# Eight modulation sums tied behind the score scalings of heads three and four, and three convolution tiles paced over the blocks of three heads, in a one-core decoder layer

## The chip, the cores and the metric

The kernel runs on one core of a Trainium2 chip. The core has five engines with queues of their own that work at the same time: TensorE (PE in the profile) multiplies matrices into PSUM, VectorE (DVE), ScalarE (ACT) and GpSimd (POOL) work on tiles, and SyncE (SP) only issues loads and stores. ScalarE's queue issues loads as well. Each engine takes its instructions in a fixed order; an instruction waits for semaphores of other engines or of a load. The metric is the device time of one execution in microseconds.

## The reference

One decoder layer on 512 positions of 1024 channels: a conditioned mixer and a conditioned convolutional feed-forward part. Cut to what matters here:

```python
cond = jax.nn.silu(c)
mod = cond @ ada_w[l] + ada_b[l]                      # 6 x 1024 modulation values
sh1, sc1, g1, sh2, sc2, g2 = jnp.split(mod[:, None, :], N_MOD, axis=-1)
u = rms_norm(x, mix_pre_g[l]) * (1.0 + sc1) + sh1
proj = u @ w_in[l]                                    # q, k, v, o, gates, glu
...
h = mlstm_chunkwise(heads(q), heads(k), heads(v), ...)          # 4 heads of 256
h = rms_norm(h, ml_norm_g[l].reshape(H, Dh)).reshape(Bsz, S, D_ML)
h = (h * jax.nn.sigmoid(o_pre)).astype(x.dtype)
y = causal_dwconv(a * jax.nn.sigmoid(gt), cv_dw_w[l], cv_dw_b[l])   # 31 taps
y = jax.nn.silu(layer_norm(y, cv_ln_g[l], cv_ln_b[l]))
mix = jnp.concatenate([h, y], axis=-1) @ w_out[l]
x = x + g1 * rms_norm(mix, mix_post_g[l])
```

The change touches how the 1024 values of `g1` are computed in time (eight blocks of 128) and when the depthwise convolution `y` is computed (eight tiles of 128 channels, 31 taps each). Both results stay what they were.

## The kernel before

All tensors lie with channels on 128 partitions and the 512 positions along the free axis; a product is made of three matrix multiplies of high and low parts (`mm3`, L201), so TensorE has most of the work. Its order is written out by hand: the glu projections, the value projection of head 0, the six projections q, q, k, k, o, o of head 0 (`head_proj`, tiles `qko`), and then a loop over h = 0, 1, 2 in which the attention of head h is laced with the projections of head h + 1. After the loop come the attention of head 3 laced with the first half of the output projection (`mixa`), its second half (`mixb`), and the feed-forward part (`up`, `dn`). The order on SyncE is by hand too. On VectorE, ScalarE and GpSimd a planner places the instructions by their priorities (work under `tc.cur_priority += LATER` comes when the engine has nothing more urgent) and by the order ties that the code adds (`behind`, and the dependency inside `ada_block`). An order tie is no wait of its own: it only says which of two instructions comes first on the engine.

The names that the prediction uses:

- `attention(h)` is a generator. It makes the four score blocks `s` (L519), which VectorE multiplies into the decay tiles `E` (L520, "score scaling"; `last_e[0]` holds the latest one), then the four outputs `o` (L530), which ScalarE copies out to `hn` (L534). VectorE scales `hn` by `fac` (L548), for which GpSimd computes a power (`fac`, L545). After that the two transposes `hT` (L554) go through PSUM, and VectorE multiplies them into `so` (L556). Scores, outputs and transposes share two PSUM banks (`atbank`), so each next one waits until the one before the last has been read out. The transposes of heads 0 and 1 are made one head later, between the first and the second pair of scores.
- `conv_tile(j)` makes one convolution tile: 25 taps on VectorE (L735, tiles `cv`), five taps on ScalarE and GpSimd (`cs`, L729 and L731), then the copy to `gt` (L742), an addition on GpSimd (L744), and the running mean and squares (`ydl`, `ysum`, `ysq`). The first `FREE` tiles are laid out whole at low priority. The others come through `pace()`, five taps at a time, each fifth tap tied behind the latest scaling or projection tap.
- `ada_block(i, behind)` makes one modulation sum: ScalarE's queue issues a load of 512 KB (L165, tiles `ada`, two buffers in turn), and VectorE multiplies it by the condition and sums along the row into `mod` (L167, the discarded product is called `junk`). A load into one of the two buffers waits for the sum that read it two blocks earlier. Blocks 16 to 23 are `g1`; `gain(0, ...)` uses them.
- `norm_rows()` normalises the eight convolution tiles: VectorE multiplies (L795), ScalarE applies silu (L796) and makes the high part `yh` (L798), VectorE makes the low part `yl` (L799).

Of the kernel before, what the change touches and what calls it, by code (L numbers as in the profile page):

```python
# [20 lines left out]
KT = D // P  # L21
# [6 lines left out]
LATER = 100000  # L28
# [26 lines left out]
def decoder_layer(ctx, tc, w_glu0, x, c, adaT, vecs, w_glu, w_qko, w_v0, w_v, w_out, w_up, w_down, out):  # L55
# [115 lines left out]
    def ada_done(a, b):  # L171
        V.tensor_tensor(out=mod[:, a:b], in0=mod[:, a:b], in1=vcols("ada_b", a, b - a), op=ALU.add)
# [320 lines left out]
    def head_proj(h, i):  # L493

        pieces, qs, ks, so = heads[h]
        ps = mmbank(f"qko{h}_{i}")
        proj(ps, pieces, i * KT)
        e = 2 * h + i % 2
        if i < 2:
            qs.append(conv4(ps, e, f"q{h}_{i}"))  # L500
        elif i < 4:
            ks.append(conv4(ps, 8 + e, f"k{h}_{i}"))
        else:
            t = slot(f"so{h}_{i}")
            S.activation(t, ps, AF.Tanh, scale=0.5)
            so.append(t)

    last_lo = [None]
    last_e = [None]
# [156 lines left out]
    def gain(i, first, g):  # L666
        V.scalar_tensor_tensor(out=gains[:, i * KT : (i + 1) * KT], in0=mod[:, first : first + KT], scalar=RD, in1=vcols(g, 0, KT),
                               op0=ALU.mult, op1=ALU.mult)
# [45 lines left out]
        tc.add_manual_dep(ins.ins, anchor.ins.name, mybir.DependencyInfo(mybir.DependencyClass.NoSync, mybir.DependencyReason.DATA),  # L714
                          reason="order on an engine")

    last_tap = [None, None]

    def conv_tile(j, every=CK):

        cp = cvbank(f"cv{j}")
        w = lambda tap: cvw[:, tap * KT + j : tap * KT + j + 1]
        S.activation(cp, cvx[j], AF.Identity, bias=vcol("cv_dw_b", j), scale=w(CK - 1))  # L723
        side = None
        for d in range(1, SIDE + 1):
            t = cvs.tile([P, T], F32, tag="cvs", name=f"cs{j}_{d}")
            if d == 1:
                V.memset(t[:, :d], 0.0)
            S.activation(t[:, d:], cvx[j][:, : T - d], AF.Copy, scale=w(CK - 1 - d))  # L729
            if side is not None:  # L730
                G.tensor_tensor(out=side[:, d:], in0=side[:, d:], in1=t[:, d:], op=ALU.add)  # L731
            else:
                side = t
        for n, d in enumerate(range(SIDE + 1, CK)):
            tap = V.scalar_tensor_tensor(out=cp[:, d:], in0=cvx[j][:, : T - d], scalar=w(CK - 1 - d), in1=cp[:, d:], op0=ALU.mult, op1=ALU.add)  # L735
            if every < CK and n % every == 0:
                behind(tap, last_e[0])
            last_tap[j // (KT - 1)] = tap
            if (n + 1) % every == 0 and d < CK - 1:
                yield  # L740
        y = cvx[j]
        S.activation(y, cp, AF.Copy)  # L742
        if side is not None:
            G.tensor_tensor(out=y, in0=y, in1=side, op=ALU.add)  # L744
        ys[j] = y

        if j:
            mean_of = ys[0] if j == 1 else ysum
            dl = cvtile(f"ydl{j}")
            V.scalar_tensor_tensor(out=dl, in0=mean_of, scalar=-1.0 / j, in1=y, op0=ALU.mult, op1=ALU.add)  # L750
            dst = ysq if j == 1 else dl
            S.activation(dst, dl, AF.Square, scale=(j / (j + 1.0)) ** 0.5)
            if j > 1:
                G.tensor_tensor(out=ysq, in0=ysq, in1=dl, op=ALU.add)
            G.tensor_tensor(out=ysum, in0=mean_of, in1=y, op=ALU.add)

    FREE = 6
    tc.cur_priority += LATER
    for j in range(FREE):
        for _ in conv_tile(j):  # L760
# [10 lines left out]
    def pace():  # L771
        tc.cur_priority += LATER
        next(paced, None)
        tc.cur_priority -= LATER
# [27 lines left out]
    for h in range(H - 1):  # L802
        head_load(h + 1)
        steps = attention(h)
        if h == 0:
            head_proj(1, 0)
        next(steps)
        head_proj(h + 1, 1 if h == 0 else 0)
        if h:
            pace()  # L810
            for _ in turns:
                pass
        next(steps)
        if h:
            pace()
            head_proj(h + 1, 1)
            pace()
        head_proj(h + 1, 2)
        if h:
            pace()  # L820
        next(steps)
        head_proj(h + 1, 3)
        if h:
            pace()
        next(steps)
        if h:
            pace()
        head_proj(h + 1, 4)
        next(steps)
        if h:  # L830
            pace()
        head_proj(h + 1, 5)
        make_E(h + 1)
        if h == H - 2:
            norm_mean()
        values = make_v(h + 1)
        next(values)
        next(values)
        if h < H - 2:
            turns = steps  # L840
        else:
            for _ in steps:
                pass
        if h == H - 2:
            norm_sums()

    tc.cur_priority += LATER
    for i in range(16, 24):
        ada_block(i, last_tap[0])
    ada_done(16, 24)  # L850
    tc.cur_priority -= LATER
    gain(0, 16, "mix_post_g")
    wo = {}
    steps = attention(H - 1)
    next(steps)
    mix_first(0)
    next(steps)
    norm_rows()
    mix_first(1)
    mix_first(2)  # L860
# [212 lines left out]
    for i in range(NF):  # L1073
# [29 lines left out]
        else:  # L1103
# [5 lines left out]
            if i % 2:  # L1109
# [7 lines left out]
                j = i // 2  # L1117
# [163 lines left out]
```

## Time and profile before

| what | value |
|---|---|
| time, median of 3 runs | 786.99 us (786.05 to 787.44) |
| the profiled execution's own time | 786.12 us |
| its span, first to last instruction | 784.1 us |
| granted TensorE clock, mean | 0.994 |
| busy share PE, DVE, ACT, POOL | 98 %, 71 %, 51 %, 66 % |

Times in the rows are microseconds from the start of the span. A row of the timeline has the start, the duration, the engine, the line and the tiles (out <- in); in brackets stands how long the engine sat idle before and what ended that. "ACTq" is ScalarE's queue at the moment when it issues a load. A row of a table by stretches has, for each engine, the busy time and the number of instructions, then the granted clock (PEclk), the share of the DMA engines and GB/s.

### The profile page before, as it was taken

What the parts mean: (1) busy time and instruction counts of PE and PEld (TensorE: products, weight loads), DVE (VectorE), ACT (ScalarE), POOL (GpSimd) and SP (SyncE); (2) the same over time, 40 slices, a digit from 0 to 9 for tenths busy, and PEclk for the clock granted to TensorE, in tenths of its full rate; (3) what the DMA queues carried; (4) which work ended last, traced back from release to release, by engine and by line L of the source; (5) the groups of instructions that cost most, each with busy time, mean ns of one, the idle gap of its engine ahead of it and who ended that gap; (6) DMA issues with size and microseconds to landing.
All of it is one profiled execution on the core that took longest, in us unless ns stands there. A gap on an engine that the chain in (4) does not pass through costs nothing.

```text
span 784.1 us, 10647 instructions
## 1 busy us (share of the span) xinstructions
PE 765.9 (98%) x3718; PEld 641.1 (82%) x3718; DVE 555.3 (71%) x817; ACT 403.5 (51%) x759; POOL 517.3 (66%) x422
## 2 busy tenths in 40 slices
PE   8999999999999799999999999999999999999996
PEld 6788898878888678888888998888888888888885
DVE  6669999997399785565868797566465567753534
ACT  6685438658555545482244444444343345646532
POOL 4689759868835946334661458687777884588870
PEclk9999999999999989999999999999999999999999
DMA  8963214222132542424953763468677573776715
GB/s 327 339 263 135 81 55 162 81 67 112 37 135 75 184 126 99 144 79 158 394 177 124 249 214 112 164 217 287 210 253 256 188 261 108 282 267 223 274 34 187
DMA packets 43897, 140.01 MB, mean 179 GB/s; under 512 B 4770, under 2 KB 6082, under 8 KB 37572
## 3 DMA queue, kind: packets, MB, share of 16 engines
q1 hardware_dynamic: 20772, 90.30, 32.4%
q10 hardware_dynamic: 23072, 49.04, 18.3%
q8 instruction: 29, 0.48, 0.3%
q14 instruction: 24, 0.20, 0.1%
HBM read 122.13 MB, written 17.19 MB: 178 GB/s over the span
## 4 chain that ended last, share of the span: by engine, by line
PE 88%; ACT 3%; DVE 3%; DMA 2%; issue 2%; POOL 1%; DVEq 0%; ACTq 0%; POOLq 0%
PE up L201 31%; PE qko L201 14%; PE dn L201 13%; PE glu L201 7%; PE mixa L201 6%; PE mixb L201 5%; PE v L201 4%; PE o L530 2%; PE s L519 2%; PE glu L347 2%; DMA ada<-in_adaT 1%; DVE cv L735 1%; DMA wglu<-in_w_glu 1%; DVE junk L167 1%; PE cps L150 0%
## 5 line engine op out<-in xcount | busy, mean ns | idle before, releaser
L735 DVE SCALAR_TENSOR_TENSOR cv<-gt,cvw,cv 128x502 f32<-128x502 f32 (+21 forms) x200 | 136.2, 728 | 2.4 <-ACT cv L723 1.3
L731 POOL TENSOR_TENSOR cs<-cs,cs 128x510 f32<-128x510 f32 (+3 forms) x32 | 44.0, 1375 | 2.7 <-ACT cs L729 2.7
L167 DVE SCALAR_TENSOR_TENSOR junk<-ada,cb 128x1024 bf16<-128x1024 f32 x20 | 32.3, 1615 | 8.8 <-DMA ada<-in_adaT 8.7
L201 PE MATMUL up<-u2l,wup_0h 128*128 128x512 f32 (+1 forms) x100 | 36.5, 365 | 0.2 <-DVE u2l L944 0.2
L201 PE MATMUL up<-u2h,wup_0h 128*128 128x512 f32 (+1 forms) x100 | 36.6, 366 | 0.0
L201 PE MATMUL up<-u2h,wup_1024h 128*128 128x512 f32 (+1 forms) x100 | 36.4, 364 | 0.0
L183 POOL TENSOR_TENSOR wup_1024l<-wup,wup_1024h 128x512 fp32r<-128x512 f32 x20 | 29.2, 1462 | 10.8 <-ACT wup_1024h L182 10.8
L201 PE MATMUL up<-u2h,wup_0l 128*128 128x512 f32 (+1 forms) x100 | 36.4, 364 | 0.0
L201 PE MATMUL up<-u2h,wup_1024l 128*128 128x512 f32 (+1 forms) x100 | 36.4, 364 | 0.0
L201 PE MATMUL up<-u2l,wup_512h 128*128 128x512 f32 (+1 forms) x100 | 36.4, 364 | 0.0
L201 PE MATMUL up<-u2l,wup_1536h 128*128 128x512 f32 (+1 forms) x100 | 36.4, 364 | 0.0
L201 PE MATMUL up<-u2h,wup_512h 128*128 128x512 f32 (+1 forms) x100 | 36.4, 364 | 0.0
L201 PE MATMUL up<-u2h,wup_1536l 128*128 128x512 f32 (+1 forms) x100 | 36.4, 364 | 0.0
L201 PE MATMUL up<-u2h,wup_512l 128*128 128x512 f32 (+1 forms) x100 | 36.4, 364 | 0.0
L201 PE MATMUL up<-u2h,wup_1536h 128*128 128x512 f32 (+1 forms) x100 | 36.4, 364 | 0.0
L201 PE MATMUL up<-u2l,wup_1024h 128*128 128x512 f32 (+1 forms) x100 | 36.4, 364 | 0.0
L183 POOL TENSOR_TENSOR wup_0l<-wup,wup_0h 128x512 fp32r<-128x512 f32 x20 | 26.9, 1347 | 8.2 <-ACT wup_0h L182 8.2
L183 POOL TENSOR_TENSOR wup_512l<-wup,wup_512h 128x512 fp32r<-128x512 f32 x20 | 28.8, 1442 | 4.8 <-ACT wup_512h L182 4.8
L183 POOL TENSOR_TENSOR wup_1536l<-wup,wup_1536h 128x512 fp32r<-128x512 f32 x20 | 30.1, 1503 | 2.8 <-ACT wup_1536h L182 2.6
L729 ACT ACTIVATE cs<-gt,cvw 128x511 f32<-128x511 f32 (+4 forms) x40 | 27.2, 713 | 5.9 <-POOL cs L731 4.0
L1050 DVE TENSOR_TENSOR b<-b,b 128x512 f32<-128x512 f32 x9 | 11.0, 1219 | 21.0 <-DMA b<-in_w_down 21.0
L327 DVE SCALAR_TENSOR_TENSOR junk<-ada,cps 128x1024 bf16<-128x1024 f32 x16 | 19.5, 1219 | 8.8 <-DMA ada<-in_adaT 4.3
(1049 smaller groups left out, 2750.5 us busy)
## 6 DMA issues: line engine op xcount, KB each, us to landing
wup<-in_w_up SPq DMA_DIRECT2D x22, 1024.0 KB, 4.9
wqko<-in_w_qko SPq DMA_DIRECT2D x12, 1024.0 KB, 4.7
ada<-in_adaT ACTq DMA_DIRECT2D x20, 512.0 KB, 4.6
b<-in_w_down ACTq DMA_DIRECT2D x36, 256.0 KB, 4.2
spillt<-b ACTq DMA_DIRECT2D x36, 256.0 KB, 2.8
ada<-in_adaT SPq DMA_DIRECT2D x16, 512.0 KB, 7.3
wo<-in_w_out SPq DMA_DIRECT2D x8, 1024.0 KB, 4.8
spare<-in_adaT ACTq DMA_DIRECT2D x12, 512.0 KB, 8.6
```

The costliest lines, as they stand in the source:

```text
L167: t = V.scalar_tensor_tensor(out=junk, in0=r, scalar=1.0, in1=cb, op0=ALU.mult, op1=ALU.mult, accum_out=mod[:, i : i + 1])
L183: (eng or G).tensor_tensor(out=lo[:, :n], in0=src, in1=hi[:, :n].bitcast(F32), op=ALU.subtract)
L201: PE.matmul(ps, l, r, start=start and i == 0, stop=stop and i == 2, skip_group_check=again)
L327: V.scalar_tensor_tensor(out=junk, in0=first[k][:, i * D : (i + 1) * D], scalar=1.0, in1=cps, op0=ALU.mult, op1=ALU.mult, accum_out=part[: ...
L347: PE.matmul(ps, blk(wk, i)[a], u[k][b], start=k == 0 and p == 0, stop=k == KT - 1 and p == 1)
L519: PE.matmul(sp[:, :n], ks[d][:, cc * P : (cc + 1) * P], qs[d][:, cc * P :], start=d == 0, stop=d == 1)
L530: PE.matmul(o[:, : DH + 2], E[h][cc][:, a : a + P], vs[h][cc], start=cc == 0, stop=cc == tt)
L729: S.activation(t[:, d:], cvx[j][:, : T - d], AF.Copy, scale=w(CK - 1 - d))
L731: G.tensor_tensor(out=side[:, d:], in0=side[:, d:], in1=t[:, d:], op=ALU.add)
L735: tap = V.scalar_tensor_tensor(out=cp[:, d:], in0=cvx[j][:, : T - d], scalar=w(CK - 1 - d), in1=cp[:, d:], op0=ALU.mult, op1=ALU.add)
L1050: V.tensor_tensor(out=b11, in0=b12, in1=b11, op=ALU.subtract)
```

## The change

`FREE` goes from 6 to 5: tile 5 is no longer laid out whole, but paced with tiles 6 and 7. The calls of `pace()` that stood under `if h:` are now made for h = 0 too, so that the paced taps are spread over three blocks and not over two. The eight sums of `g1`, which were tied behind the last tap of tile 6 (`last_tap[0]`), are split: blocks 16 to 19 are tied behind the score scaling that is the latest after the second step of the loop's block (for h = 2 the last of the third head), and blocks 20 to 23 behind the last score scaling of the fourth head, after the second step of the last attention. The addition of the bias and the gain move along with them.

```diff
-    FREE = 6
+    FREE = 5
...
         head_proj(h + 1, 1 if h == 0 else 0)
+        pace()
         if h:
-            pace()
             for _ in turns:
                 pass
         next(steps)
+        scaled = last_e[0]
+        pace()
         if h:
-            pace()
             head_proj(h + 1, 1)
             pace()
         head_proj(h + 1, 2)
-        if h:
-            pace()
+        pace()
         next(steps)
...
     tc.cur_priority += LATER
-    for i in range(16, 24):
-        ada_block(i, last_tap[0])
-    ada_done(16, 24)
+    for i in range(16, 20):
+        ada_block(i, scaled)
     tc.cur_priority -= LATER
-    gain(0, 16, "mix_post_g")
     wo = {}
     steps = attention(H - 1)
     next(steps)
     mix_first(0)
     next(steps)
+    tc.cur_priority += LATER
+    for i in range(20, 24):
+        ada_block(i, last_e[0])
+    ada_done(16, 24)
+    gain(0, 16, "mix_post_g")
+    tc.cur_priority -= LATER
     norm_rows()
```

The remaining calls of `pace()` in the loop lose their `if h:` in the same way. TensorE and SyncE keep their order to the last instruction; VectorE, ScalarE and GpSimd do not. Three places matter.

VectorE around the transposes of head 1 (`hT1`), before; `junk_18` to `junk_23` are modulation sums, `E20` and `E21` the score scalings of head 2, `so1_4` and `so1_5` the reads of the two transposes:

```order
L548 TENSOR_SCALAR hn1_0_2391<-hn1_0_2391,fac1_2516,rd1_2515 128x256 x2
L548 TENSOR_SCALAR hn1_1_2392<-hn1_1_2392,fac1_2516,rd1_2515 128x256 x2
L167 SCALAR_TENSOR_TENSOR junk_18_3224,mod_136<-ada_18_3222,cb_109 128x1024
L735 SCALAR_TENSOR_TENSOR cv7_2457<-gt7_984,cvw_137,cv7_2457 128x497
L167 SCALAR_TENSOR_TENSOR junk_19_3228,mod_136<-ada_19_3226,cb_109 128x1024
L167 SCALAR_TENSOR_TENSOR junk_20_3232,mod_136<-ada_20_3230,cb_109 128x1024
L520 SCALAR_TENSOR_TENSOR E20_2563<-s2_0_2753,E20_2563 128x512
L167 SCALAR_TENSOR_TENSOR junk_21_3236,mod_136<-ada_21_3234,cb_109 128x1024
L520 SCALAR_TENSOR_TENSOR E21_2564<-s2_1_2757,E21_2564 128x384
L167 SCALAR_TENSOR_TENSOR junk_22_3240,mod_136<-ada_22_3238,cb_109 128x1024
L167 SCALAR_TENSOR_TENSOR junk_23_3244,mod_136<-ada_23_3242,cb_109 128x1024
L556 SCALAR_TENSOR_TENSOR so1_4_1979<-so1_4_1979,hT1_0_2797 128x512
```

The same place now:

```order
L548 TENSOR_SCALAR hn1_0_2403<-hn1_0_2403,fac1_2521,rd1_2520 128x256 x2
L548 TENSOR_SCALAR hn1_1_2404<-hn1_1_2404,fac1_2521,rd1_2520 128x256 x2
L520 SCALAR_TENSOR_TENSOR E20_2568<-s2_0_2758,E20_2568 128x512
L520 SCALAR_TENSOR_TENSOR E21_2569<-s2_1_2762,E21_2569 128x384
L556 SCALAR_TENSOR_TENSOR so1_4_1979<-so1_4_1979,hT1_0_2802 128x512
L556 SCALAR_TENSOR_TENSOR so1_5_2049<-so1_5_2049,hT1_1_2812 128x512
```

All six sums have left the stretch between the scaling of `hn1` and the reads of the transposes; sums 16 to 19 now come after the last scaling of head 2, each with its load.

VectorE in the normalisation of the convolution tiles, now (before, the two `gt` rows, `yl0`, `yl1` and `yl2` followed one another, and no sum stood among them):

```order
L520 SCALAR_TENSOR_TENSOR E31_3040<-s3_3_3272,E31_3040 128x128
L167 SCALAR_TENSOR_TENSOR junk_20_3278,mod_136<-ada_20_3276,cb_109 128x1024
L792 TENSOR_TENSOR gt0_623<-gt0_623,ry_b_3298 128x512
...
L792 TENSOR_TENSOR gt7_984<-gt7_984,ry_b_3298 128x512
L167 SCALAR_TENSOR_TENSOR junk_21_3282,mod_136<-ada_21_3280,cb_109 128x1024
L796 TENSOR_TENSOR yl0_3306<-gt0_623,yh0_3305 128x512
L796 TENSOR_TENSOR yl1_3312<-gt1_626,yh1_3311 128x512
L167 SCALAR_TENSOR_TENSOR junk_22_3286,mod_136<-ada_22_3284,cb_109 128x1024
L796 TENSOR_TENSOR yl2_3318<-gt2_629,yh2_3317 128x512
L167 SCALAR_TENSOR_TENSOR junk_23_3290,mod_136<-ada_23_3288,cb_109 128x1024
L796 TENSOR_TENSOR yl3_3324<-gt3_700,yh3_3323 128x512
```

Sums 20 to 23 stand here now, the first ahead of all eight multiplications, the last after `yl2`.

ScalarE at the copies out of the first two outputs of head 3 (`hn3_0`, which free the two PSUM banks), before:

```order
L182 ACTIVATE wo0_3_1024h_3654<-wo0_3_3644 128x512
L798 ACTIVATE yh4_3329<-gt4_771 128x512
L533 ACTIVATE dm3_3418<-o3_0_3421 128x1
L798 ACTIVATE yh5_3335<-gt5_842 128x512
L533 ACTIVATE dm3_3418<-o3_1_3427 128x1
L798 ACTIVATE yh6_3341<-gt6_913 128x512
L798 ACTIVATE yh7_3347<-gt7_984 128x512
L534 ACTIVATE hn3_0_3419<-o3_0_3421 128x256
```

The same place now, from the high part of tile 2 on:

```order
L165 DMA ada_23_3288<-in_adaT 128x1024
L182 ACTIVATE wo0_3_512h_3650<-wo0_3_3644 128x512
L165 DMA ada_28_3574<-in_adaT 128x1024
L795 ACTIVATE yh3_3323<-gt3_700 128x512
...
L795 ACTIVATE yh4_3329<-gt4_771 128x512
L533 ACTIVATE dm3_3418<-o3_0_3421 128x1
L533 ACTIVATE dm3_3418<-o3_1_3427 128x1
L795 ACTIVATE yh5_3335<-gt5_842 128x512
L165 DMA ada_29_3578<-in_adaT 128x1024
L795 ACTIVATE yh6_3341<-gt6_913 128x512
L795 ACTIVATE yh7_3347<-gt7_984 128x512
L534 ACTIVATE hn3_0_3419<-o3_0_3421 128x256
```

Three loads of modulation blocks have come into this stretch (a fourth, of block 22, stands ahead of the first silu). That of block 29 goes into the buffer that `junk_23` reads, and it stands ahead of `hn3_0`. Before, these loads were issued during the block of h = 2.

More of the change, by code (lines that the diff above doesn't have):

```diff
@@ L715, in behind @@
                           reason="order on an engine")
-    last_tap = [None, None]
     def conv_tile(j, every=CK):
@@ L737, in conv_tile @@
                 behind(tap, last_e[0])
-            last_tap[j // (KT - 1)] = tap
             if (n + 1) % every == 0 and d < CK - 1:
@@ L818, in decoder_layer @@
         head_proj(h + 1, 2)
-        if h:
-            pace()
+        pace()
         next(steps)
         head_proj(h + 1, 3)
-        if h:
-            pace()
+        pace()
         next(steps)
-        if h:
-            pace()
+        pace()
         head_proj(h + 1, 4)
         next(steps)
-        if h:
-            pace()
+        pace()
         head_proj(h + 1, 5)
```

## The prediction

> **What bounds the kernel now.** I read the page's first part, then who waited for whom on TensorE.
>
> ```profile
> PE 765.9 (98%) x3718; PEld 641.1 (82%) x3718; DVE 555.3 (71%) x817; ACT 403.5 (51%) x759; POOL 517.3 (66%) x422
> PE s L519 <- DVE so L556: 5.9, 2, 5.6
> PE cps L150 <- ACT crow L149: 2.9, 1, 2.9
> PE glu L347 <- ACT uh L388: 1.0, 1, 1.0
> ```
>
> TensorE sets the end, and its order stays as it is, so only its waits can change. In the stretch that the change touches there is one: the scores wait 5.6 us for `so`. The same passage comes twice, for head 0 without a long wait and for head 1 with it. TensorE's timeline shows both from the transposes to the first outputs, and the stretches give the clock.
>
> ```profile
> 214.52 1.03 PE L554 MATMUL hT<-ident,hn 128*128 128x128 f32 x8
> 228.23 1.03 PE L530 MATMUL o<-v,E 128*128 128x258 f32 x4
> 269.23 1.03 PE L554 MATMUL hT<-ident,hn 128*128 128x128 f32 x8
> 275.83 1.22 PE L519 MATMUL s<-q_0c,k_2c 128*128 128x256 f32 x2 [5.56 <-DVE so L556]
> 290.31 1.03 PE L530 MATMUL o<-v,E 128*128 128x258 f32 x4
> 273.40:274.00 0.60, 0.00 (x0) 0.00 (x0) 0.60 (x1) 0.07 (x1) 0.60 (x1) 0.56 0.97 335
> 274.00:275.80 1.80, 0.00 (x0) 0.00 (x0) 1.80 (x4) 0.00 (x0) 1.80 (x2) 0.50 0.50 182
> 280.00:280.50 0.50, 0.50 (x3) 0.38 (x2) 0.50 (x2) 0.00 (x0) 0.00 (x0) 0.70 0.43 172
> ```
>
> Head 0 takes 228.23 - 214.52 = 13.71, head 1 takes 290.31 - 269.23 = 21.08. The difference, **7.37 us, is what the wait costs**: 5.2 more idle, and the rest clock. The granted clock falls to 0.50 near 273.47, which is 3.2 into the idle time, and is back near 280.3: about 4.5 us of matmuls at half speed lose 2.2. Why `so` was late, VectorE's timeline tells.
>
> ```profile
> 255.85 2.10 DVE L548 TENSOR_SCALAR hn<-hn,fac,rd 128x256 f32<-128x256 f32 x4
> 264.10 1.92 DVE L167 SCALAR_TENSOR_TENSOR junk<-ada,cb 128x1024 bf16<-128x1024 f32 x1 [2.77 <-DMA ada<-in_adaT]
> 269.73 2.02 DVE L167 SCALAR_TENSOR_TENSOR junk<-ada,cb 128x1024 bf16<-128x1024 f32 x1 [0.97 <-DMA ada<-in_adaT]
> 273.14 2.03 DVE L167 SCALAR_TENSOR_TENSOR junk<-ada,cb 128x1024 bf16<-128x1024 f32 x1 [1.38 <-DMA ada<-in_adaT]
> 275.10 0.68 DVE L556 SCALAR_TENSOR_TENSOR so<-so,hT 128x512 f32<-128x512 f32 x1
> DMA to landing us min/median/max: 3.7/3.8/4.5
> 268.70 0.63 ACT L182 ACTIVATE wqko_1024h<-wqko 128x512 fp32r<-128x512 f32 x1 [3.67 <-DVE junk L167]
> ```
>
> VectorE waits for load after load with the transposes ready since 270.3: two buffers, 3.8 us from issue to landing, and the next load only once a sum has freed its buffer. The last row (ScalarE) shows the other side: a load that waits for its buffer holds up everything behind it on ScalarE's queue.
>
> **The change, part by part.**
>
> *Sums 16 to 23 leave head 1's transposes.* The reads of `hT1` then stand right behind `E21`. For them to be on time `hn1` must be scaled before 269.2. The slowest link is GpSimd's power behind a weight split.
>
> ```profile
> 249.73 1.29 POOL L183 TENSOR_TENSOR wqko_512l<-wqko,wqko_512h 128x512 fp32r<-128x512 f32 x1 [1.44 <-ACT wqko_512h L182]
> 253.53 2.04 POOL L545 TENSOR_TENSOR fac<-ssq,mhalf 128x4 f32<-128x4 f32 x1
> L548 DVE TENSOR_SCALAR hn<-hn,fac,rd x14: 398/408/1493, 199.0 to 360.0; 128x256 f32<-128x256 f32 x14
> ```
>
> The additions of tile 6 and the first side taps of tile 7 now precede that split, about 2.5 us, so the power ends near 256 to 258; four scalings at the slowest 1.49 make it 264. Slack at least 5 us. I take the passage at head 0's length: **-7.37**. It is at most this (a wait of 0.34 stays in head 0's too), and zero at worst.
>
> *Sums 16 to 19 behind head 2's scalings.* They fall into the projections that follow the scores. Four sums at 1.5 for five taps at 0.73 that move forward: VectorE some 2.4 us later, against 4.6 idle further on.
>
> ```profile
> L735 DVE SCALAR_TENSOR_TENSOR cv<-gt,cvw,cv 128x502 f32<-128x502 f32 (+21 forms) x200 | 136.2, 728 | 2.4 <-ACT cv L723 1.3
> 305.99 0.47 DVE L540 TENSOR_TENSOR dm<-dm,em 128x4 f32<-128x4 f32 x1 [4.64 <-ACT dm L533]
> ```
>
> ScalarE is held by its loads here too. On the old scale without the wait, sum 16 ends near 275.4 (five us of reads, scalings and taps behind `hT`), the load of block 18 lands 3.8 later, and its sum frees the buffer for block 20 near 281, sum 19 that for block 21 near 284. The first outputs of head 2 are there from 290.31 - 7.37 = 282.9 on, and their banks are wanted a projection of 24 matmuls later, so 284 is early enough. **0**; without that cover it would be the 3.67 of the row above.
>
> *Tile 5 paced, tiles 6 and 7 earlier.* 25 taps leave the head of the loop's first block. About ten of them land between the outputs of head 0 and `E10`, 7.3 us, where VectorE idled:
>
> ```profile
> 195.45 0.69 DVE L750 SCALAR_TENSOR_TENSOR ydl<-ysum,gt 128x512 f32<-128x512 f32 x1 [1.79 <-POOL gt L744]
> 208.01 0.69 DVE L520 SCALAR_TENSOR_TENSOR E<-s,E 128x512 f32<-128x512 f32 x1 [5.68 <-PE s L519]
> ```
>
> 7.5 us of idle time hold them, and `E10` is not wanted before the transposes at 214.5. **0**; with the cover gone VectorE would be late by what the taps exceed it, and TensorE only beyond 6 us more.
>
> *Sums 20 to 23 inside the normalisation.* Here the loads meet ScalarE's queue again. The rows, in order ScalarE, VectorE, TensorE, and the DMA engines in the stretch:
>
> ```profile
> 332.50 1.28 ACT L796 ACT_TABLE_LOAD   x1
> 334.94 1.52 ACT L796 ACTIVATE gt<-gt,vec 128x512 f32<-128x512 f32 x2 [1.16 <-DVE gt L795]
> 342.69 0.62 ACT L798 ACTIVATE yh<-gt 128x512 fp32r<-128x512 f32 x1
> 346.66 1.15 ACT L798 ACTIVATE yh<-gt 128x512 fp32r<-128x512 f32 x2
> 347.71 0.65 ACT L534 ACTIVATE hn<-o 128x256 f32<-128x256 f32 x2
> 332.88 0.74 DVE L520 SCALAR_TENSOR_TENSOR E<-s,E 128x256 f32<-128x256 f32 x2 [3.08 <-PE s L519]
> 369.94 1.23 DVE L167 SCALAR_TENSOR_TENSOR junk<-spare,cb 128x1024 bf16<-128x1024 f32 x1
> 344.95 1.47 PE L530 MATMUL o<-v,E 128*128 128x258 f32 x6
> 348.99 1.47 PE L530 MATMUL o<-v,E 128*128 128x258 f32 x6
> 345.00:350.00 5.00, 5.00 (x24) 4.23 (x23) 3.90 (x5) 4.73 (x14) 1.74 (x3) 1.00 0.00 0
> ```
>
> `o3_2` (348.99) takes the bank that `hn3_0` frees, today at 348.1: 0.9 to spare. Now, on the same scale: `junk_20` runs 333.55 to 334.8; the load of block 22, which reuses its buffer, waits for that and is issued by 335.15. The table load (1.28) stands behind it and no longer hides in the wait for the first `gt`: the first silu starts at 336.5, not 334.94. The row of `yh2` starts 7.75 behind the first silu, so at 344.25, and the load of block 23 is issued with it, 344.3. It lands 3.8 later, 348.1; `junk_23` ends 1.27 later, near 349.45. Only then may the load of block 29 be issued, to 349.75, and behind it come `yh6`, `yh7` (0.52 each, from the row of two) and `hn3_0` (0.38). The bank is free at 351.2: **TensorE loses about 2.25** at `o3_2`. Bounds: with the load at 3.7 and the sum at its fastest 1.21, 2.1; with the load at 4.72 and the sum at its slowest 2.2, 4.1.
>
> ```profile
> 268.32 4.72 DMA ada<-in_adaT
> L167 DVE SCALAR_TENSOR_TENSOR junk<-ada,cb x12: 1207/1514/2196, 250.2 to 387.4; 128x1024 bf16<-128x1024 f32 x12
> ```
>
> I take 3.8 and 1.23, since the stretch has idle DMA engines and little GpSimd work. TensorE's idle time is 0.4 shorter than its loss (the running matmul ends at 349.4), so 1.9, under the 3.2 after which the clock fell. Nothing behind it is late: `yl3` follows at 350.5, and its tile is multiplied only after `o3_2`, `o3_3` and three other tiles.
>
> [...]
>
> *Sum:* -7.37 + 2.25 = **-5.1**. On the profiled execution's own 786.12 (784.1 of span and 2.0 around it) that is 781.0. The median of the three runs is 0.87 above that execution, so I predict 786.99 - 5.1 = **781.9**.
>
> **The rivals.**
>
> *No wait at `o3_2`: 779.6.* If ScalarE reaches `hn3_0` before 349, the whole 7.37 stays. It needs 2.25 us less in a chain of which 3.8 is a load and 1.27 a sum, both at their fastest rows already. Against: the rows add up without gaps. For: I know the order, not the gaps.
>
> *The new wait crosses the clock's limit: 785.8.* At the upper bound TensorE loses 4.1, idles 3.7, the clock halves as at 273.47 and costs up to 2.2: -7.37 + 6.3 = -1.1. It decides from a loss of 3.6, that is a load and a sum together 1.35 slower than I take them. For: sums took 1.9 to 2.0 beside GpSimd's work at 264 to 275. [...]
>
> *Slower, 788.9: the load of block 23 is slow.* Four loads of the same size issued together took a median of 8.6 here:
>
> ```profile
> spare<-in_adaT ACTq DMA_DIRECT2D x12, 512.0 KB, 8.6
> ```
>
> With 8.6 for 3.8 the loss is 2.25 + 4.8 + 2.2 = 9.3, net +1.9. It outweighs the gain from a landing of about 6.7 on. For: the load of 1 MB for `wo1_0`, which follows a split of ScalarE, moves later by the 1.5 us of the silu and may still run when block 23 is asked for. Against: the row 345 to 350 shows nothing moving.
>
> *The change doesn't do what it says: about 787.* The wait at `hT1` stays in part because `hn1` comes late, past 269.2. It needs 5 us beyond my slowest count, with TensorE's loss at `o3_2` added.
>
> **How the numbers follow.** Forecast 0.55; no new wait 0.17; the clock's limit 0.13; the slow load 0.08; `hn1` late 0.05; 0.02 for what I don't see. A measurement of this kernel tells about 0.2 %, 1.6 us, from no change. Faster by more (under 785.4) are the forecast, the first rival and a fifth of the second: 0.75. Within 0.2 %: the rest of the second and most of the late `hn1`: 0.14. Slower: 0.11. The forecast's own range is 780.0 (loss 0.4) to 783.8 (loss 4.1 with the clock held); the range is 779.0 to 786.0, which takes in the first two rivals, about 0.85.
>
> **What would show it.** Right: no row of `s` waiting for `so` above 0.4, the passage from `hT` to `o` 13.7 in head 1 too, granted clock 1.00 there; one new wait of TensorE, `o` on ScalarE's `hn`, 1.9 idle, in the passage that now begins near 345 - 7.4; ahead of it a load issue of ScalarE's queue that waits for `junk`, and a `junk` that waits for its load. Wrong: a wait of `s` that stays; that wait of `o` absent, or with a clock of 0.50 behind it; any wait of TensorE between 160 and 260.

## The result, and the profile after

| what | before | changed |
|---|---|---|
| first comparison, median of 4 runs each | 787.22 us (786.05 to 787.75) | 779.47 us (777.74 to 781.14) |
| ratio, 95 % interval | | 0.9903 [0.9879, 0.9928] |
| second comparison (run "again" below; 17 and 6 runs) | 787.30 us | 781.78 us (780.20 to 783.19) |
| ratio, 95 % interval | | 0.9924 [0.9901, 0.9946] |
| profiled execution of the first comparison, its span | 786.12, 784.1 us | 779.11, 777.3 us |

The change makes the kernel faster, by 7.75 us in the first comparison and by 5.5 in the second. The intervals overlap between 5.7 and 7.8 us. The prediction was 5.1 less, and 781.9.

Who waited for whom on TensorE, in the changed kernel (us in total, times, longest):

```profile
PE cps L150 <- ACT crow L149: 3.1, 1, 3.1
PE s L519 <- ACT E L611: 1.1, 1, 1.1
PE o L530 <- ACT hn L534: 0.7, 1, 0.7
PE s L519 <- DVE so L556: 0.7, 2, 0.3
```

The 5.6 us for which the scores waited for `so` are gone. In their place stand two smaller waits: `o` for ScalarE's `hn`, which was forecast, and `s` for ScalarE's `E`, which was not. TensorE's timeline of the changed kernel shows where they lie:

```profile
158.57 0.91 PE L519 MATMUL s<-q_0c,k_2c 128*128 128x384 f32 x2 [1.07 <-ACT E L611]
267.96 1.04 PE L554 MATMUL hT<-ident,hn 128*128 128x128 f32 x8
269.34 0.70 PE L519 MATMUL s<-q_0c,k_2c 128*128 128x256 f32 x2 [0.34 <-DVE so L556]
281.67 1.47 PE L530 MATMUL o<-v,E 128*128 128x258 f32 x6
336.31 1.47 PE L530 MATMUL o<-v,E 128*128 128x258 f32 x6
341.22 1.57 PE L530 MATMUL o<-v,E 128*128 128x258 f32 x6 [0.71 <-ACT hn L534]
```

Head 1 now takes 281.67 - 267.96 = 13.71 from `hT` to `o`, the length of head 0, and the wait there is 0.34. From `o3_0` to `o3_2` it takes 4.91, 0.87 more than before. The chain of waits through that passage, in order of time (start, us, what):

```profile
333.02 4.98 DMA ada<-in_adaT
338.10 1.24 DVE junk L167 x2
339.37 0.33 ACTq L165
339.75 0.59 ACT yh L795
340.81 0.37 ACT hn L534
341.22 1.57 PE o L530 x6
```

This is the forecast chain, link by link: the load of block 23, its sum, the issue of the load that reuses the buffer, `yh` and `hn3_0` behind that issue, `o3_2`. The same marks on TensorE, as differences of start times, divide the span into passages. They are made from the profiled executions of before, of the first comparison and of "again". `fcum` (L619) is the product that sums the forget gates; what lies ahead of it is called the opening here. `o3_0` and `o3_2` are the first and the third output of head 3:

| passage | before | changed, first | changed, again |
|---|---|---|---|
| start to `fcum` | 128.30 | 126.17 | 127.65 |
| `fcum` to `hT` of head 0 | 86.22 | 87.07 | 87.06 |
| `hT` of head 1 to its neighbour `o2_0` | 21.08 | 13.71 | 13.70 |
| `o2_0` to `hT` of head 2 | 33.36 | 33.35 | 33.36 |
| `o3_0` to `o3_2` | 4.04 | 4.91 | 6.14 |
| `o3_2` to `mixb` | 31.37 | 31.47 | 31.47 |
| `mixb` to `up` | 45.47 | 45.84 | 45.47 |
| `up` to `dn` | 243.60 | 244.05 | 244.34 |

The three passages that are not in the table (`hT` of head 0 to that of head 1, `hT` of head 2 to `o3_0`, `dn` to the end) agree within 0.02. The differences to before add up to -6.9 in the first profile and to -4.2 in the second.

Two rows are no work of this change. Up to `fcum` nothing in the order of the engines was edited, and over 14 profiles of these kernels its start lay between 126.17 and 128.66. `up` to `dn` lay between 243.58 and 245.91. The profile of before had one of the latest openings and the first profile of the change the earliest: that is 2.1 of its 6.9. The 0.37 of `mixb` to `up` in the first profile is not in "again" either: a copy into `gains` took 1.33 there and 0.16 in the two others, and `gT` (L653), which reads them, waited 0.23.

### The profile page after: what moved, and what is told of

It reads as the page before. It is cut to its first block, busy times and chain, and to the rows that moved or that the text cites. A ratio compares the mean times of both kernels' runs of the same rounds, so it can differ in the third digit from the quotient of the medians.

```text
span 777.3 us, 10639 instructions
## 1 busy us (share of the span) xinstructions
PE 763.5 (98%) x3718; PEld 638.9 (82%) x3718; DVE 556.1 (72%) x817; ACT 403.8 (52%) x759; POOL 510.9 (66%) x422
## 4 chain that ended last, share of the span: by engine, by line
PE 78%; DVE 8%; DMA 4%; ACT 4%; issue 3%; POOL 1%; ACTq 0%; DVEq 0%; POOLq 0%
PE up L201 28%; PE dn L201 13%; PE qko L201 12%; PE glu L201 7%; PE v L201 6%; PE mixb L201 3%; PE o L530 2%; PE s L519 2%; PE mixa L201 2%; DMA spare<-in_adaT 2%; PE glu L347 2%; DVE cv L733 2%; DVE junk L167 1%; DMA wglu<-in_w_glu 1%; DMA ada<-in_adaT 1%
## 5 line engine op out<-in xcount | busy, mean ns | idle before, releaser
L733 DVE SCALAR_TENSOR_TENSOR cv<-gt,cvw,cv 128x488 f32<-128x488 f32 (+22 forms) x200 | 138.0, 729 | 2.9 <-ACT cv L721 1.3
L729 POOL TENSOR_TENSOR cs<-cs,cs 128x510 f32<-128x510 f32 (+3 forms) x32 | 41.7, 1304 | 0.1
L167 DVE SCALAR_TENSOR_TENSOR junk<-ada,cb 128x1024 bf16<-128x1024 f32 x20 | 30.4, 1520 | 4.7 <-DMA ada<-in_adaT 4.6
L1048 DVE TENSOR_TENSOR b<-b,b 128x512 f32<-128x512 f32 x9 | 13.9, 1543 | 21.9 <-DMA b<-in_w_down 21.9
L183 POOL TENSOR_TENSOR wqko_1024l<-wqko,wqko_1024h 128x512 fp32r<-128x512 f32 x12 | 15.5, 1290 | 16.3 <-PE v L201 9.1
```

Source lines behind the costliest of these rows:

```text
L167: t = V.scalar_tensor_tensor(out=junk, in0=r, scalar=1.0, in1=cb, op0=ALU.mult, op1=ALU.mult, accum_out=mod[:, i : i + 1])
L183: (eng or G).tensor_tensor(out=lo[:, :n], in0=src, in1=hi[:, :n].bitcast(F32), op=ALU.subtract)
L1048: V.tensor_tensor(out=b11, in0=b12, in1=b11, op=ALU.subtract)
```

## The experiments

Differences are to the kernel before in the same session, of medians; the profiles' passages, which leave opening and feed-forward part out, are the sharper measure. In some variants the added lines shift line numbers by a few.

### The change again

No edit.

> The changed kernel, unchanged, beside the kernel before in one session. By the sum of its waits (hT1 -7.4, the wait of s on E of head 0 with the taps' new order +0.85, o3_2 between +0.9 and +2.1 as in two profiles) it is 4.4 to 5.7 under the kernel before. Rival, the 7.75 of the first comparison comes again: then 2 to 3 us are gained at a place that I have not found.

Measured: 781.78 against 787.30, -5.5. TensorE's waits in this run:

```profile
PE o L530 <- ACT hn L534: 1.9, 1, 1.9
PE s L519 <- ACT E L611: 1.1, 1, 1.1
PE s L519 <- DVE so L556: 0.7, 2, 0.3
```

The sum of waits holds, the rival does not: no further gain of 2 to 3 us is there to be found. And `o3_2` now waits 1.93, which was the forecast, where the first profile had 0.71. Whatever decides between the two is not in the program, since both profiles are of the same kernel.

### One half at a time

Only the sums (tiles and pacing as before):

```diff
-    FREE = 5
+    FREE = 6
...
-        pace()
+        if h:
+            pace()
```

> The eight sums are split as in the change, the taps stay as in the kernel before (six whole tiles, two paced in two blocks). If the move of the sums is the whole gain: no row of s waiting for so above 0.4, head 1's passage from hT to o 13.7, the wait of o3_2 about 0.7 as in the change, and 779.5; and if the 1.07 us for which s waited on E of head 0 (158.6 in the change's trace) comes from the new order of the taps, that wait is gone and the time is 778.5. Rival, the taps carry part of it (with tile 7 not yet done VectorE has no room for four sums in head 3's projections): a wait of s or of a qko bank of 2 to 4 us in head 2's block, 781 to 783.

Measured: 781.19 against 786.13, ratio 0.993 [0.9906, 0.9954], -4.9. Head 1's passage is 13.70, `o3_0` to `o3_2` 6.14 (a wait of 1.93), `fcum` to `hT` 86.27 with a wait of `s` of 0.17. So the whole gain at `hT1` is the move of the sums, and VectorE had room for them without the earlier taps. The time expected was 1.7 to 2.7 too low: I took 0.7 for the wait at `o3_2`, which is 1.2 of it, and started from the first comparison's 779.5, with its early opening.

Only the taps (the sums tied behind the last tap of tile 6, as before):

```diff
-    for i in range(16, 20):
-        ada_block(i, scaled)
+    for i in range(16, 24):
+        ada_block(i, last_tap[0])
+    ada_done(16, 24)
...
-    for i in range(20, 24):
-        ada_block(i, last_e[0])
-    ada_done(16, 24)
```

> Only the three tiles are paced over three blocks; the eight sums stay tied behind the last tap of tile 6. My prediction priced the taps at nothing, which leaves the wait for so at 5 to 6 us and the time at 787 (788 with the wait of s on E of head 0). Rival: the tie goes along with the tile, whose copy out stands at 241.54 in the change and at 250.33 before, so the sums start 8.7 earlier, end near 266 on the scale of before and are done ahead of hT1 (269.2): the wait for so is under 1, no wait at o3_2, and 779.5 to 781.

Measured: 785.07 against 786.13, ratio 0.9983 [0.9967, 0.9999]. Neither expectation came true. The wait for `so` is gone, as the rival said, but TensorE waits a step earlier, at the transposes themselves:

```profile
272.14 1.12 PE L554 MATMUL hT<-ident,hn 128*128 128x128 f32 x4 [2.71 <-DVE E L520]
274.41 0.90 PE L554 MATMUL hT<-ident,hn 128*128 128x128 f32 x3 [1.16 <-DVE E L520]
```

VectorE's timeline of that kernel tells why:

```profile
242.54 1.21 DVE L167 SCALAR_TENSOR_TENSOR junk<-ada,cb 128x1024 bf16<-128x1024 f32 x1
262.66 5.26 DVE L548 TENSOR_SCALAR hn<-hn,fac,rd 128x256 f32<-128x256 f32 x4
270.26 1.21 DVE L167 SCALAR_TENSOR_TENSOR junk<-ada,cb 128x1024 bf16<-128x1024 f32 x1
271.41 0.68 DVE L520 SCALAR_TENSOR_TENSOR E<-s,E 128x512 f32<-128x512 f32 x1
```

The eight sums still last 29 us, from 242.5 to 271.5. They now stand ahead of `hn1`'s scalings and of `E20`, whose bank the transposes need. The stall moved with the sums: TensorE waits 3.9 there in place of 5.6, and head 1's passage takes 17.21. Pacing the tiles does not remove it while the sums stay tied behind the taps.

### Where the loads stand on ScalarE's queue

The loads of blocks 24 to 39 tied behind `hn3_1`:

```diff
-        nc.scalar.dma_start(r, adaT[...])
+        ld = nc.scalar.dma_start(r, adaT[...])
+        if 24 <= i < 40:
+            tc.add_manual_dep(ld.ins, last_hn[13].ins.name, ... NoSync ...)
```

> The change, with the loads of blocks 24 to 39 tied on ScalarE's queue behind the copy hn3_1, so that no load stands ahead of hn3_0 that waits for block 23's sum. If the wait at o3_2 comes from the load of block 29 in that queue: o3_0 to o3_2 is 4.04 as before, no wait of o on hn, 0.9 less than the change, 778.6. Rival, ScalarE is late by its own work (eight silus, yh, splits) in the normalisation: the wait stays at 0.5 or more and the time within 0.3 of the change.

Measured: 779.89 against 786.13, ratio 0.9912 [0.9889, 0.9935], -6.2. No wait of `o` on `hn`; `o3_0` to `o3_2` is 4.09. The load of block 29, which has nothing to do with `hn3_0`, was what held it up. ScalarE's own work does not. Not all of the -6.2 is due to this edit: in this profile the wait of `s` on `E` is missing too (`fcum` to `hT` 85.82), for a reason that comes further down.

The load of block 23 made to wait until `yh2` is done:

```diff
+            done = S.activation(hi, ys[j], AF.Copy)
+            if j == 2:
+                tc.add_manual_dep(held[0].ins, done.ins.name, ... Sync ...)
```

> The change, with the load of block 23 made to wait until yh2 has been executed, which is where it stands in ScalarE's order and when I predicted its issue. In the change it was issued at 333.02, 2.7 before yh2 started. If that early issue is what made the loss 0.87 and not 2.25: issue near 336.3, landing 3.7 to 5.0 later, loss at o3_2 1.7 to 3.0, time 0.8 to 2.1 above the change, 780.3 to 781.6. Rival, the loss is set by ScalarE's own work: loss 0.9, time as the change. In the order that results the load of block 29 stands behind yh7, right ahead of hn3_0.

Measured: 781.63 against 786.13, -4.5; loss at `o3_2` 2.10 with a wait of 1.9. That is inside what I expected, and yet it decides nothing, since "again" has the same 2.10 with the load issued early. ScalarE's timeline shows the issue where the edit put it:

```profile
337.18 0.61 ACT L798 ACTIVATE yh<-gt 128x512 fp32r<-128x512 f32 x1
337.70 0.61 ACT L185 ACTIVATE wo_512h<-wo 128x512 fp32r<-128x512 f32 x1
337.82 0.34 ACTq L166 DMA_DIRECT2D ada<-in_adaT  x1
...
343.11 0.33 ACTq L166 DMA_DIRECT2D ada<-in_adaT  x1
343.49 0.66 ACT L537 ACTIVATE hn<-o 128x256 f32<-128x256 f32 x2 [1.91 <-DVE junk L170]
```

But the planner also moved two `yl` ahead of the sum on VectorE, and `yh6` and `yh7` ahead of block 29's load on ScalarE, so more than one thing changed.

### Who comes first, the sum or GpSimd's split

GpSimd's split `wo_1024l` made to wait for the sum of block 23:

```diff
+        if name == "wo0_3_1024":
+            tc.add_manual_dep(low.ins, sums[23].ins.name, ... Sync ...)
```

> The change, with GpSimd's split wo_1024l made to wait for the sum of block 23, so that the two never meet. In the profiles with a wait of 1.93 at o3_2 that split started 0.4 to 0.7 ahead of the sum, the sum took 1.7 to 1.9 and ended 1.08 behind the split; in those with 0.7 the sum came first, took 1.23, and the split took 2.32. If it is who comes first at the port that makes the difference of 1.2: the sum takes 1.2 to 1.3 here, the wait at o3_2 is 0.7 (loss 0.9) and at most what a slower landing adds, 1.2, never 1.93. Rival, the landing alone makes it (4.98 against 5.5 to 5.7, with the sum's start): the wait is 1.9 in this run if the load lands after 5.5. TensorE uses wo_1024l only 1.2 behind o3_2, so its delay costs nothing. The time is that of the change less 0 to 1.2, which the rounds can hardly tell.

Measured: the sum takes 1.23, the wait is 0.80, the loss 0.96; 780.87 against 786.03. Without the edit two cases are seen. First GpSimd's split and VectorE's sum in the first profile of the change:

```profile
338.16 2.32 POOL L183 TENSOR_TENSOR wo_1024l<-wo,wo_1024h 128x512 fp32r<-128x512 f32 x1
...
338.10 1.23 DVE L167 SCALAR_TENSOR_TENSOR junk<-ada,cb 128x1024 bf16<-128x1024 f32 x1 [1.05 <-DMA ada<-in_adaT]
```

Then the same two in "again":

```profile
339.64 1.30 POOL L183 TENSOR_TENSOR wo_1024l<-wo,wo_1024h 128x512 fp32r<-128x512 f32 x1
...
340.30 1.72 DVE L167 SCALAR_TENSOR_TENSOR junk<-ada,cb 128x1024 bf16<-128x1024 f32 x1 [1.77 <-DMA ada<-in_adaT]
```

The one that starts second takes longer and ends about 1.1 behind the first: the split takes 2.32 where it takes 1.30 as the first, and ends 1.15 behind the sum's end (339.33); or the sum takes 1.72 where it takes 1.23 as the first, and ends 1.08 behind the split's end (340.94). The split starts 1.85 or 1.86 behind `o3_0` in the profiles without the edit. "again", "sums_only" and "mhl_pool" have the sum second: it starts 2.52, 2.31 and 2.38 behind `o3_0`, but ends at 4.24 in all three, so the loss is 2.10 in each. The first profile and "eight_norm" have it first, and lose 0.87 and 0.86. The rows show the delay and not what makes it: "the port" of the expectations is my name for it, and no run shows one.

Who comes first is settled by the landing of block 23's load: 4.98 and 4.97 after its issue where the sum is first, 5.50 to 5.71 where it is second. From the first profile to "again" the sum starts 0.73 later and takes 0.49 longer, so the later landing is the larger part of the 1.2, and the meeting with the split adds the rest. The edit does not separate the two well: the load landed early in it too (5.07), and the sum started at 1.88, where the split would have come at about the same moment.

### The wait of `s` on `E`

`Mhl`, a subtraction of two small tiles, on GpSimd:

```diff
-    V.tensor_tensor(out=Mhl[LO : LO + H, :], in0=Mr, ...
+    G.tensor_tensor(out=Mhl[LO : LO + H, :], in0=Mr, ...
```

> The change, with the subtraction Mhl (L632, 4x512) on GpSimd. On VectorE it took 3.88 in the change, 1.74 before, and ended 0.55 behind the last of a row of GpSimd additions each time. If that late end is what delays k_3c, ScalarE's E of head 0 and so the second score block: no wait of s on E at 158, from fcum to hT0 86.2 and not 87.1, 0.85 less than the change. Rival, the taps' new order on ScalarE does it by itself: the wait stays near 1.1, same time.

Measured: 781.31 against 787.30, ratio 0.991 [0.9881, 0.994]. No wait of `s` on `E`; `fcum` to `hT` is 85.71, against 87.06 in "again". The taps' order is that of the change but for a few neighbours, so the order alone does not make the wait. VectorE's row in the change, and GpSimd's beside it:

```profile
143.87 3.88 DVE L632 TENSOR_TENSOR Mhl<-Mr,Mhl 4x512 fp32r<-4x512 f32 x1
...
143.41 1.29 POOL L183 TENSOR_TENSOR wqko_1024l<-wqko,wqko_1024h 128x512 fp32r<-128x512 f32 x1
144.66 1.30 POOL L741 TENSOR_TENSOR gt<-gt,cs 128x512 f32<-128x512 f32 x1
145.92 1.28 POOL L183 TENSOR_TENSOR wqko_1536l<-wqko,wqko_1536h 128x512 fp32r<-128x512 f32 x1
```

`Mhl` ends at 147.75, 0.55 behind the third of GpSimd's additions (147.20). It lasted through three of them in a row (143.41 to 147.20). In all eleven profiles that have it on VectorE it ends 0.54 to 0.56 behind a GpSimd addition. In four of them (the kernel before, "sums_only", "loads_late", "eight_norm") it ends while a further one runs, which takes 1.73 to 1.75 in place of 1.3. What decides that stays open.

The taps of `k_3c` stand behind it on VectorE, their silu ahead of `E` on ScalarE, and the second score block needs the bank that `E` reads. But the late end is only half of the cause: in the kernel before, `Mhl` ended 22.17 behind `fcum`, later than the 21.58 of the change, and no such wait is listed. The other half is ScalarE's order. Its rows before, then in the change:

```profile
148.19 1.93 ACT L729 ACTIVATE cs<-gt,cvw 128x511 f32<-128x511 f32 x3
152.63 0.63 ACT L480 ACTIVATE k_3c<-k_3c 128x512 f32<-128x512 f32 x1 [2.51 <-DVE em L639]
158.03 0.56 ACT L611 ACTIVATE E<-Mb,ga 128x384 f32<-128x384 f32 x1
...
149.91 0.63 ACT L480 ACTIVATE k_3c<-k_3c 128x512 f32<-128x512 f32 x1 [4.91 <-DVE k_3c L479]
151.98 1.93 ACT L727 ACTIVATE cs<-gt,cvw 128x511 f32<-128x511 f32 x3
156.76 0.56 ACT L611 ACTIVATE E<-Mb,ga 128x384 f32<-128x384 f32 x1
```

Three side taps (`cs`, 1.93) stood ahead of the silu of `k_3c`, where ScalarE had idle time left. With the tiles paced as in the change they stand behind it and ahead of `E`, so `E` comes 6.85 behind the silu in place of 5.40. Over all profiles, in us:

| `Mhl` on VectorE | its end behind `fcum` | silu of `k_3c` to `E` | kernels | wait of `s` on `E` |
|---|---|---|---|---|
| 1.14 | 19.62 | 6.85 | loads_late, eight_norm | none |
| 1.74 to 1.75 | 22.17 to 22.21 | 5.40 | before, sums_only | none; 0.17 |
| 3.17 | 22.86 | 5.40 | both_off | 0.92 |
| 3.86 to 3.91 | 21.57 to 21.63 | 6.84 to 6.85 | change (twice), taps_only, load23_yh2, eight_h2, split_behind_sum | 1.07 to 1.14 |
| on GpSimd | 18.59 to 18.67 | 7.34 to 7.35 | mhl_pool, pool_late, pool_six_two | none |

With either order of the taps the wait comes when `Mhl` ends late, and the change's order leaves it 1.45 less room. "loads_late" and "eight_norm" pace the taps as the change does and have no wait, so the wait is not in every execution of that order.

This run had a surprise at `o3_2`. The wait is the 1.93 of "again", but here the clock fell. The stretches of TensorE's clock (last columns but two: granted clock):

```profile
342.50:343.00 0.50, 0.18 (x1) 0.19 (x2) 0.50 (x2) 0.50 (x3) 0.00 (x0) 1.00 1.13 352
343.00:343.50 0.50, 0.50 (x3) 0.45 (x3) 0.50 (x3) 0.50 (x3) 0.00 (x0) 0.87 0.89 254
343.50:344.00 0.50, 0.50 (x3) 0.41 (x2) 0.50 (x1) 0.50 (x4) 0.37 (x1) 0.50 0.57 229
346.50:347.00 0.50, 0.50 (x3) 0.37 (x2) 0.00 (x0) 0.00 (x0) 0.00 (x0) 0.72 0.49 115
```

TensorE resumed at 342.82. The clock went to half only at 343.37 (from the 0.87) and came back at 346.78 (from the 0.72), 3.41 later. `o3_2` to `mixb` took 33.09 for 31.47, so this cost 1.6 and ate what the edit had gained.

Both new waits taken off by other means, the edits of "sums_only" and "loads_late" in one kernel:

```diff
-    FREE = 5
+    FREE = 6
...
+        if 24 <= i < 40:
+            tc.add_manual_dep(ld.ins, last_hn[13].ins.name, ... NoSync ...)
```

> Both new waits taken away: taps as before (six whole tiles), sums split as in the change, loads of blocks 24 to 39 behind hn3_1 on ScalarE's queue. If the sum of the waits holds: no wait of s on E above 0.2, none at o3_2, 7.4 under the kernel before and 2 to 2.5 under the change in the same session. Rival, tile 7's later taps keep VectorE busy in head 3's projections and something else is late: less than 1 under the change.

Measured: 780.55 against 787.30, ratio 0.9904 [0.988, 0.9928], -6.75, and 1.2 under the change in that session. `o3_2` no longer waits (4.10), but `s` waits 0.92 with the old order of the taps, `Mhl` 3.17. It is half a miss: I had put that wait down to the order of the taps alone. With the old order it comes too, when `Mhl` meets GpSimd for 3.17 and ends 22.86 behind `fcum`.

### Other splits of the eight sums

All eight behind head 2's scalings:

```diff
-    for i in range(16, 20):
+    for i in range(16, 24):
         ada_block(i, scaled)
```

> The change, with all eight sums behind the scalings of head 2, none in the normalisation. By the loads' own chain on ScalarE (issues near 274, 277, 280, 283, then 286.5, 288.5, 291.6 and 293.5 for the two of blocks 28 and 29) each is issued before ScalarE's next reader of a qko bank is wanted: no wait of a qko bank, none at o3_2, the wait of s on E of head 0 stays, 6.5 under the kernel before. Rival, the eight loads hold ScalarE up (3.67 at a time as at head 1 before): a wait of qko on ScalarE or of s on so in head 2's block of 2 us or more, 3 to 5 under the kernel before.

Measured: 786.10 against 787.30, ratio 0.9973 [0.9956, 0.9991]: most of the gain is gone, and my expectation with it. The wait has a place that I had not named, the mean over the convolution tiles. ScalarE, GpSimd and TensorE:

```profile
300.42 0.60 ACT L505 ACTIVATE so<-qko 128x512 f32<-128x512 f32 x1 [2.86 <-DVE junk L167]
301.43 0.59 ACT L739 ACTIVATE gt<-cv 128x512 f32<-128x512 f32 x1
...
306.15 1.26 POOL L752 TENSOR_TENSOR ysum<-ysum,gt 128x512 f32<-128x512 f32 x1
...
307.47 1.28 PE L776 MATMUL ytot<-ysum,ones 128*128 128x512 f32 x2 [3.65 <-POOL ysum L752]
```

The load of block 29 was issued near 300, not near 293.5, because four of the sums took 1.8 to 2.4 and VectorE's taps came between. Tile 7's copy stands behind it, and behind the copy `ysum`. `o2_0` to `hT2` takes 38.78, 5.4 more: the wait of 3.65, and a granted clock of 0.50 from 308.30 to 311.72. So four sums fit there, eight don't: the nothing that I had priced for step 2 holds for four and ends before eight.

All eight in the normalisation:

```diff
-    for i in range(16, 20):
-        ada_block(i, scaled)
...
-    for i in range(20, 24):
+    for i in range(16, 24):
         ada_block(i, last_e[0])
```

> The change with all eight sums behind the scalings of head 3, so none beside head 2's projections. The chain to hn3_0 is the same as in the change (block 19 in the place of block 23): o3_2 waits 0.7 to 1.9 again. Behind it the loads of blocks 22, 23 and 28 wait for sums between the copies of o3_2 and o3_3 on ScalarE; I work out hn3_3 0.4 later and hT3 ready at 356.2 against 358.0 wanted, so nothing more: time of the change, within 0.8. Rival, every pair of sums in the normalisation costs a landing: a wait of hT3 or o3_3 of 3 to 5, time 3 to 7 above the change. If the time is below the change instead, the four sums in head 2's projections were not free.

Measured: 782.51 against 787.00, ratio 0.9939 [0.9916, 0.9962]. `o3_0` to `o3_2` is 4.90 (wait 0.70), `o3_2` to `mixb` 31.49. `mixb` to `up` takes 46.14, 0.67 more than before, and `gT` waits 0.5 of it for `gains`. Eight sums there cost no more at `o3_2` than four, and taking the four out of head 2's projections gained nothing: `o2_0` to `hT2` is 33.35.

### Versions without the new waits

`Mhl` on GpSimd and the late loads together:

```diff
-    V.tensor_tensor(out=Mhl[LO : LO + H, :], in0=Mr, ...
+    G.tensor_tensor(out=Mhl[LO : LO + H, :], in0=Mr, ...
...
+        if 24 <= i < 40:
+            tc.add_manual_dep(ld.ins, last_hn[13].ins.name, ... NoSync ...)
```

> The change with Mhl on GpSimd and the loads of blocks 24 to 39 behind hn3_1: all three waits off (so at hT1, E of head 0 at the second score block, hn at o3_2). By the sum -7.4 for hT1 and -0.5 for fcum to hT0 (85.7 in the run with Mhl on GpSimd, 86.2 before): 7.9 under the kernel before, about 779.3 against 787.2. Rival, a part of the sum is given back in the feed-forward part: 6 to 7 under.

Measured: 777.15 against 787.00, ratio 0.9879 [0.9857, 0.99], -9.9. Neither wait is there. `fcum` to `hT` is 85.81, `o3_0` to `o3_2` 4.09, `up` to `dn` 243.59. Its passages behind the opening sum to 7.6 under before, near the expected 7.9; the rest of the 9.9 lies in the spread of openings and runs. It has the lowest median of the kernels, 4.3 below the change by the differences to before in two sessions. Its interval, 7.9 to 11.3 us under before, just misses that of "again" (4.3 to 7.8); it does meet that of the first comparison (5.7 to 9.5). The two were not run side by side.

`Mhl` on GpSimd, six sums and two, no load tied:

```diff
-    V.tensor_tensor(out=Mhl[LO : LO + H, :], in0=Mr, ...
+    G.tensor_tensor(out=Mhl[LO : LO + H, :], in0=Mr, ...
...
-    for i in range(16, 20):
+    for i in range(16, 22):
...
-    for i in range(20, 24):
+    for i in range(22, 24):
```

> The change with Mhl on GpSimd and the sums split six and two: blocks 22 and 23 alone in the normalisation, both loaded ahead of it, so that the loads of blocks 28 and 29 wait for no landing; no load is tied. If it is the landing of block 23 inside the normalisation that makes o3_2 wait: no wait there, 4.04 from o3_0 to o3_2. VectorE has two sums more in head 2's block; with eight the last tap came at 300.5 and ytot waited 3.65 for ysum, with six I work out 297 and a ysum near 303.3 against 303.8 wanted: no wait or one up to 0.5. 7.4 to 7.9 under the kernel before. Rival, the port and the queue make the taps later than that: ytot waits 1 to 3, 4.5 to 6.5 under.

Measured: 778.84 against 787.00, ratio 0.9898 [0.9878, 0.9918], -8.2. `o3_0` to `o3_2` is 4.10 and `o2_0` to `hT2` 33.36: no wait at `ytot` either. With both loads of the normalisation ahead of it, nothing in its chain waits for a landing. This reaches by the split alone what the other version needs a tie for.

## Why the prediction was right, and where it was not

- *Sums leave head 1's transposes, -7.37.* Measured -7.37 and -7.38 in the two profiles of the change, with a granted clock of 1.00 there in both, and a passage of 13.70 to 13.71 in every variant but one. That one ("taps_only") kept the old tie and kept a stall.
- *Sums 16 to 19 behind head 2's scalings, 0.* Right: `o2_0` to `hT2` is unchanged. The cover was thinner than my reason said. I looked for the end of it on ScalarE; with eight sums it ended at `ysum`.
- *Taps, 0.* This step failed: it cost +0.85 in both profiles of the change. I had looked for cover on VectorE alone, and only between the outputs of head 0 and `E10`. What I left out is ScalarE, where three side taps moved ahead of `E`, and GpSimd's additions, 0.54 to 0.56 behind one of which `Mhl` ends each time. The two together make the wait; where `Mhl` ends early, as in "loads_late" and "eight_norm", the step costs nothing. I had said that a wait of TensorE between 160 and 260 would show the forecast wrong; this one stands at 158.57, just ahead of that stretch, and is a miss all the same.
- *Sums 20 to 23 in the normalisation, +2.25, 1.9 idle.* From the load on, the mechanism is right in every link; what starts the load is not. The size is right in "again" (2.10 and 1.93) and 1.4 too large in the first profile. That it is right in "again" is luck: the load went out earlier than I thought and landed later, and the two errors nearly cancelled. On the scale of the first profile (8.64 earlier, from the row of `E`) I had the first silu at 327.86; it came at 327.96. I had the load of block 23 at 335.66, with `yh2`; it was issued at 333.02:

```profile
332.37 0.80 ACT L793 ACTIVATE gt<-gt,vec 128x512 f32<-128x512 f32 x1
333.02 0.33 ACTq L165 DMA_DIRECT2D ada<-in_adaT  x1
333.07 1.51 ACT L793 ACTIVATE gt<-gt,vec 128x512 f32<-128x512 f32 x2
334.49 0.61 ACT L182 ACTIVATE wo_0h<-wo 128x512 fp32r<-128x512 f32 x1
335.01 0.80 ACT L793 ACTIVATE gt<-gt,vec 128x512 f32<-128x512 f32 x1
...
335.71 0.61 ACT L795 ACTIVATE yh<-gt 128x512 fp32r<-128x512 f32 x1
```

  In ScalarE's order the load stands behind that last row, `yh2`. It went 2.6 ahead: it waited for the sum of block 21, which freed its buffer at 332.99, and not for `yh2`. Its landing took 4.98 in place of 3.8, in "again" 5.71, and the sum 1.24 or 1.74 in place of 1.27. I had counted on idle DMA engines, but SyncE had issued a load of 1 MB for `wo` at 331.93, and from 334 to 337 the engines moved 393 to 422 GB/s. That may be what made the landing longer; no run separates it.
- *The sum, -5.1, and 781.9.* By the passages that the change touches it is -7.37 + 0.85 + 0.9 or 2.1 + 0.1, that is -5.5 or -4.3. In the first profile the forecast of -5.1 comes so near because two errors have opposite signs: +0.85 for the taps, and 1.4 less than forecast at `o3_2`. In "again" only the first of them is left. The forecast time of 781.9 is just above both medians, 779.47 and 781.78. In the first profile 2.1 us of the gain is its opening; the other three runs of that comparison have no profile, so how much of its 7.75 is the change stays open.
- *The rivals.* The wait at `o3_2` exists, so the first one is out. The second comes to 785.9 by its own terms (-7.37 + 6.3), not 785.8. The half clock came in one of the four profiles with a wait near 1.93 ("mhl_pool"), far below the 3.2 of idle time from which I let it decide. The slow load stayed away: the landings were 5.0 to 5.7 in the profiles of the change, against the 6.7 from which I had the gain lost.

What stays open: why the load of block 23 takes 5.0 in some runs and 5.5 to 5.7 in others, why `Mhl` on VectorE takes 1.14 in some profiles and up to 3.91 in others, and why `up` to `dn` varies by 2.3.

## What to carry to other kernels

Sums that must load, wait and free a buffer belong where nothing urgent stands behind them on either engine. A load on ScalarE's queue that waited for its buffer kept ScalarE idle for 3.67 before and for 0.71 and 1.93 in the two profiles of the change, so list what is behind it before moving it. A VectorE instruction beside GpSimd's additions took up to 3.4 times its shortest length here (`Mhl` 1.14 to 3.91); price a chain through it with the long one too. Compare passages between marks, not single profiles' totals.

## What the runs showed of the hardware

Block 23's load was issued ahead of ScalarE's own execution. It went out at 333.02 with five activations that precede it in ScalarE's order still to start; it waited for its buffer (the sum ended at 332.99) and not for them. In "again" it went out at 334.50, ahead of the same five. How far ahead a load can go, no run shows. I read the order as the time of issue, and that was the error in what starts the load.

The granted clock fell after a different time in each of four kernels. It fell 3.2 after TensorE went idle in the kernel before, 2.1 after in "taps_only" (269.43 to 271.54), 2.5 after in "mhl_pool" and 4.5 after in "eight_h2", in the last two when TensorE was at work again. The idle time of 1.93 of "mhl_pool" left it alone in "again". It stayed at half for 6.83 in the kernel before (273.47 to 280.30), 6.84 in "taps_only", 3.41 in "mhl_pool" and 3.42 in "eight_h2": two lengths, the longer twice the shorter. What decides between "mhl_pool" and "again" is not shown.
